# A reordered front and first half blocks, a ring of two pairs of PSUM banks, modulation tiles in the scan, and copies one ahead in the FFN

## The chip, the cores and the metric

The kernel runs on one core of a Trainium2 chip. The metric is device time in microseconds (us) of one execution. Five engines run side by side, each through its own list of instructions in order: TensorE (PE in the rows, PEld for its weight loads), VectorE (DVE), ScalarE (ACT), GpSimd (POOL) and SyncE (SP, which only issues DMAs). They wait for each other by semaphores. Matmul results land in PSUM, eight banks of 128 partitions x 512 floats; all else is in SBUF.

## The reference

One layer of a diffusion transformer with an S5 mixer, in float32: 1024 latent tokens and 256 context tokens of width 1024.

```python
m_l = split(silu(c) @ ada_w + ada_b, 6)              # modulation of the latent tokens
m_c = split(silu(c_ctx) @ ada_w + ada_b, 6)          # and of the context tokens
h_l = rms_norm(x, norm_mix) * (1 + m_l[1]) + m_l[0]; h_c = (the same of ctx with m_c)
# S5: 64 groups of 16 channels, 64 complex states each, in two directions;
# the latent scan starts from the context's last state
lam_bar = exp(lam * exp(log_step)); b_bar = (lam_bar - 1) / lam * b
state[t] = lam_bar * state[t-1] + b_bar @ u[t];  y[t] = Re(c_mat @ state[t])     # both directions added
g = gelu(y + d_skip * h_l);  x = x + m_l[2] * (g * sigmoid(g @ w_glu + b_glu))
h = rms_norm(x, norm_ffn) * (1 + m_l[4]) + m_l[3]
x = x + m_l[5] * ((silu(h @ w1) * (h @ w3)) @ w2)    # hidden width 2816
out = rms_norm(x, norm_final)
```

## The kernel before

Time is cut into 160 chunks of 8 tokens (32 of context, 128 latent). Instructions run on each engine in the order of the Python code: nothing is rescheduled, so moving a call moves its instructions on every engine that it uses. The stages are these.

**Front.** DMAs bring `x`, the context (`ctxT`) and the first 16 modulation tiles. ACT squares ten pieces of the tokens into a ring `junk` of two buffers, POOL folds each, and PE sums them (L184). Meanwhile DVE works out `lam_bar`, its powers `PW` and the input factors `CP` (`cmul`). PE spreads `CP` over the partitions (`dup`, L289) and the result is evicted as the table `LB` (L313, L77). `ada1(h, k)` (L282) accumulates the rows of shift and scale in the bank `prow`; `mix_rows` turns them (L411, L414), and `mix_cols` makes columns `cols` and `colp` of them (L426, L427). With these `rs_lat`, `u_lat`, `u_act` and `u_ctx` normalise and modulate the inputs `U`, eight groups at a time (`b` = 0 to 7).

**Sums.** A loop over 16 half blocks, `hb` = 2*b + d (d is the direction). Each needs input weights: `bl_make(hb)` multiplies `LB` with the matrices `BXY` into two parts (on POOL for the numbers in `PMUL`, else on DVE, which then reads a copy of the `LB` slice that `lb_psum` puts into PSUM by ACT). `bl_sum` adds the parts by an accumulating DMA from POOL's queue; below `NPE` PE adds them instead (L397, L398). `bl_tr` transposes them through PSUM (L400) into the ring `Win` (L401). `sums(hb)` multiplies the weights with `U` (L516), and ACT evicts the results into the state buffer `STQ` (L521 for d = 0, L523 and L524 for d = 1). All of these take turns in one PSUM ring `pw` of three banks. `pair` and `ctx_tree` combine neighbouring chunks by rotations (`rot`, on DVE or POOL). `power8` and `powers` square `lam_bar` up to the larger strides, and `pw_full` spreads `PW` (L289, L350). Between the blocks `ada` (L470) accumulates the second part of the modulation, 64 tiles of 256 KB in the bank `pm`; the first 32 of them stand in this loop.

**Scan.** `ctx_last`, then `scan()` on DVE: 32 coarse steps, fills, 63 fine steps. Meanwhile `run(prog)` goes through a written-out list of words for the other engines: `A`n takes tiles up to number n, `C` makes output matrices (POOL, for the first four with PE, L602), `K` and `T` the Toeplitz kernels by way of DRAM (L713 to L731), `M` turns the second modulation (L778, L782), `L` and `G` load and sign the matrices `Cs`, `F` fills on POOL, `R` restacks states (L819), `P` multiplies (L837, L842) and `Y` evicts (L894).

**GLU and FFN.** Then come the gate with the last restacks, and 22 hidden tiles of the FFN in split precision (L1209 to L1211). The first two are plain; for the rest the seven combinations of `h` in `BV` are prepared by `t3_steps`, `t24_steps` and `t1_steps` beside tiles 0 and 1. Such a step copies an operand into a PSUM bank of a ring of two by ACT (L1266, L1278, L1285), DVE adds, and `t_split` casts by ACT (L1151) and subtracts on POOL. `up_plain` advances them (`rest`) between its matmuls.

Most DVE and POOL operations are recorded by the helper `tt` and have its line, L70.

```python
for hb in range(16):
    sums(hb)
    ...
    elif hb < 13:
        bl_tr(hb + 3)
    ...
HOW = ((PE,) * 4,) + ((SY,) * 4,) * 3
run("A40 C00 A44 C01 A48 C02 A52 C03 A56 A60 A64 K0 K1 L2 C10 C11 M0 M1 C12 T0 ...")
```

Of the kernel before, what the change touches and what calls it, by code (L numbers as in the profile page):

```python
# [17 lines left out]
P = 128  # L18
# [19 lines left out]
def s5_ffn_kernel(tc, a, out):  # L38
# [3 lines left out]
    with ctx:  # L42
# [80 lines left out]
        def pw(shape=(4, P)):  # L123
            return pA.tile([P] + list(shape), F32, tag="w", name="pw", bufs=3)

        prow = pA.tile([P, 512], F32, tag="r3", name="prow")
        pm = pA.tile([P, 512], F32, tag="r2", name="pm")
        V.memset(prow, 0.0)
        V.memset(pm, 0.0)
# [8 lines left out]
        ctxT = view(RA, 13.5, [G, 32])  # L138
# [21 lines left out]
        LTa = pA.tile([P, 512], F32, tag="r0", name="lta")  # L160
        LTb = pA.tile([P, 512], F32, tag="r1", name="ltb")
        lbt = pA.tile([P, 512], F32, tag="r4", name="lbt")

# [13 lines left out]
        junk = [view(RC[3], 8 + 4 * i, [2, 512]) for i in range(2)]  # L177
        psx, psc = pw([4, P]), pw([16, 32])
        for i in range(10):
            src = X[:, 8 * i:8 * i + 8] if i < 8 else ctxT[:, 32 * i - 256:32 * i - 224]  # L180
            jk, po = junk[i % 2], psx if i < 8 else psc
            S.activation(jk.rearrange("p a b -> p (a b)").rearrange("p (g c) -> p g c", c=src.shape[2]), src, AF.Square)
            tt(jk[:, 0], jk[:, 0], jk[:, 1], ADD, E)
            PE.matmul(po.rearrange("p g c -> p (g c)"), blk, jk[:, 0], start=i % 8 == 0, stop=i in (7, 9))  # L184
# [112 lines left out]
        V.tensor_reduce(rsx, psx.rearrange("p g c -> p c g"), AX.X, ADD)  # L297
        cmul(PW[:, 2:3], PW[:, 0:1])
        V.tensor_copy(yb, PW[:, 3])
        cmul(CP[:, 4:6], CP[:, 0:2])  # L300
        cmul(CP[:, 6:8], CP[:, 2:4])
        V.tensor_reduce(rsc, psc.rearrange("p g c -> p c g"), AX.X, ADD)
        S.activation(rsb, rsb, AF.Sqrt, bias=epsc[:, 0:1], scale=1.0 / D)
        LB = view(RC[2], 8, [2, T, P])
        for n in range(4):
# [4 lines left out]
            if n % 2:  # L310
                ts(o, pt, sgn[:, 0:1] if i else 1.0, MUL)
            else:
                S.activation(o, pt, AF.Copy, scale=sgn[:, 0:1] if i else 1.0)  # L313
        for k in range(3):
            ada1(0, k)
        cmul(PW[:, 7:8], PW[:, 3:4])
# [4 lines left out]
        def power8():  # L321

            pt = pw([2, 4, 2, 8])
# [10 lines left out]
        def powers(*ps_):  # L334

            t2 = view(RXc, 3, [2, G])
            for p in ps_:
                i_, o = SQ[p], SQ[p + 1]
                if p == 1:
                    V.tensor_copy(LQ[p], i_)  # L340
                j_ = LQ[p] if p < 2 else i_
                tt(t2, i_[:, 0:2], j_[:, 0::2], MUL)
                stt(o[:, 1], i_[:, 0], -2.0, j_[:, 2], MUL, MUL)
                stt(o[:, 2], i_[:, 0], 2.0, j_[:, 2], MUL, MUL)
                tt(o[:, 0], t2[:, 0], t2[:, 1], ADD)

        def pw_full(n):
            pt = pw()
            dup(pt, lambda d: PW[:, 2 * n:2 * n + 2].rearrange("p t i g -> p (t i) g"))
            S.copy(PWF[:, 2 * n:2 * n + 2].rearrange("p t i g -> p (t i) g"), pt)  # L350
# [4 lines left out]
        BL2 = [view(r, kb, [8, T, HC]) for r, kb in ((RC[1], 12), (RXc, 4), (RC[3], 4), (RA, 22), (RA, 26), (RA, 30), (RA, 34))]  # L355
        Win = [view(RC[r], kb, [4, P]) for r, kb in ((3, 0), (3, 2), (2, 0), (2, 2), (2, 4), (2, 6))]
# [17 lines left out]
        def lb_psum(*hbs):  # L374

            for hb in hbs:
                n, o = {1: (0, 0), 3: (0, 128), 4: (1, 384), 7: (0, 0), 9: (0, 128), 11: (1, 384), 12: (2, 384), 14: (0, 0),
# [11 lines left out]
        def bl_tr(hb):  # L389
            b, d = divmod(hb, 2)  # L390
            t1, t2 = bls(hb)
            for j in range(2):
                pt = pw()
                for i in range(4):
                    w = t1[:, 4 * j + i].rearrange("p s h -> p (s h)")
                    if hb < NPE:
                        PE.matmul(pt[:, i], w, ident, start=True, stop=False)  # L397
                        PE.matmul(pt[:, i], t2[:, 4 * j + i].rearrange("p s h -> p (s h)"), ident, start=False, stop=True)  # L398
                    else:
                        PE.transpose(pt[:, i], w, ident)  # L400
                S.copy(Win[(2 * hb + j) % 6], pt)  # L401
# [6 lines left out]
        r4, mx = view(RA, 38, [4, P]), view(RA, 40, [2, 2, 32])  # L408

        def mix_rows():  # L410
            S.copy(r4, prow.rearrange("p (m n) -> p m n", m=4))  # L411
            pt = pw()
            for m in range(4):
                PE.transpose(pt[:, m], r4[:, m], ident)  # L414
            return pt

        def mix_cols(h, pt):

            hs = slice(4 * h, 4 * h + 4)
# [5 lines left out]
            pcol = pw([2, 2, 32])  # L425
# [24 lines left out]
        NA = 24  # L450
        stg = [view(RA, kb, [512]) for kb in [74] + [42 + 2 * i for i in range(15)] + [60.5 + 2 * i for i in range(8)]]
        stg += [view(RC[2], 8 * (1 - i // 4) + 2 * (i % 4), [512]) for i in range(8)]
        ada_at = [0, 0]

        def ada_tile(i):
            return stg[i if i < NA else NA + (i - NA) % 8]
# [18 lines left out]
        lb_psum(1, 3, 4)  # L475
        power8()
        bl_make(0)
# [9 lines left out]
        ada1(0, 7)
        pt = mix_rows()
        bl_tr(1)
        mix_cols(0, pt)  # L490
        u_act(0, 0, 4)
        u_lat(0, 4)
        u_ctx(0)
        bl_make(3)
        rs_lat(1)
        tt(Xc[:, 16:], ctxT[:, 16:], bc(rcp, 1, G - 16), MUL)
        u_ctx(1)
        u_lat(1)
        SY.dma_start(BXY[:, 0], a["bxy"][:, 2])
        powers(0, 1)  # L500
        rs_lat(2)
        bl_make(4)
        bl_make(5)
        bl_sum(4)
        stt(KD.rearrange("p q g h -> p (q g) h"), bc(pat, 1, 16), 1.0, bc(dcol, 2, HC), MUL, MUL)
        tq = None


        def sums(hb):
            b, d = divmod(hb, 2)  # L510
            for j in range(2):
                w = Win[(2 * hb + j) % 6]
                for ri in range(2):
                    pv = pw([512])[:, 0:320].rearrange("p (e c) -> p e c", e=2)
# [999 lines left out]
```

## Time and profile before

| | |
|---|---|
| median of 3 runs | 1100.76 us (1095.19 to 1100.89) |
| the profiled execution | 1099.35 us |
| its span in the trace | 1097.1 us |
| mean granted clock of TensorE | 0.969 |
| busy: PE, DVE, ACT, POOL | 91%, 71%, 38%, 57% of the span |
| PE on the chain that ended last | 74% of the span |
| HBM read | 83.20 MB |

A row of the timeline gives start and duration in us, engine, line, operation, output and inputs with shapes, and in brackets the idle time of that engine just before and what ended it. Rows that stand next to each other and are alike are merged ("x4"). One float32 matmul of the program is two instructions in the trace. In rows of windows each engine's busy time stands in turn, then the granted clock, the share of the DMA engines' time and GB/s.

### The profile page before, as it was taken

How to read it: one execution, taken by the hardware profiler on the slowest of the kernel's cores; microseconds unless marked ns; L12 is line 12 of the kernel's file. 1: busy time of each engine (PE TensorE's matmuls, PEld its weight loads, DVE VectorE, ACT ScalarE, POOL GpSimd, SP SyncE). 2: the span in 40 equal slices, each digit the busy share in tenths (PEclk: the TensorE clock that was granted, in tenths of full speed). 3: DMA queues.
4: the chain of work that ended last, by engine and by line, in shares of the span. 5: the costliest groups of instructions: out<-in, count | busy, mean ns of one | idle time of the engine just before them, and what ended most of it. 6: DMA issues, size and time to landing. Idle time of an engine off the chain costs nothing.

```text
span 1097.1 us, 16934 instructions
## 1 busy us (share of the span) xinstructions
PE 1000.6 (91%) x6208; PEld 803.8 (73%) x6208; DVE 777.2 (71%) x1808; ACT 419.2 (38%) x880; POOL 621.8 (57%) x484
## 2 busy tenths in 40 slices
PE   5889897546999999699999999999999999999997
PEld 1546632435899997587888888888888888888875
DVE  7688989994665786588666666666666666666657
ACT  4338741543864574322222222222222222222236
POOL 4446787881273454656555555555555555555563
PEclk9989999777999999999999999999999999999999
DMA  9577778665324012001111111100111111111104
GB/s 340 210 207 154 198 238 218 166 126 126 110 95 131 22 34 83 19 1 59 58 58 58 58 58 58 54 28 35 58 58 58 58 58 58 59 58 58 52 27 153
DMA packets 54514, 103.04 MB, mean 94 GB/s; under 512 B 4384, under 2 KB 25120, under 8 KB 53408
## 3 DMA queue, kind: packets, MB, share of 16 engines
q1 hardware_dynamic: 46656, 85.57, 23.6%
q0 software_dynamic: 3456, 12.58, 6.2%
q10 hardware_dynamic: 4320, 3.81, 1.1%
q8 instruction: 49, 0.80, 0.3%
q14 instruction: 33, 0.27, 0.1%
HBM read 83.20 MB, written 6.16 MB: 81 GB/s over the span
## 4 chain that ended last, share of the span: by engine, by line
PE 74%; DMA 6%; ACT 6%; DVE 6%; POOL 5%; issue 2%; ACTq 0%; SPq 0%; POOLq 0%; DVEq 0%
PE pu L1211 11%; PE pu L1210 11%; PE pu L1209 11%; PE pd L1209 7%; PE pd L1211 7%; PE pd L1210 7%; PE pw L516 3%; PE pe L974 3%; PE pe L975 3%; PE pe L973 3%; POOL c L70 3%; DVE ru L70 2%; PE prow L282 2%; DMA rxc<-in_cxy 1%; PE pm L470 1%
## 5 line engine op out<-in xcount | busy, mean ns | idle before, releaser
L70 POOL TENSOR_TENSOR c<-rxc,c 128x512 fp32r<-128x512 f32 x128 | 166.9, 1319 | 186.9 <-ACT c L1151 179.8
L70 DVE TENSOR_TENSOR ru<-pd,ru 128x512 f32<-128x512 f32 x336 | 226.6, 689 | 0.6 <-PE pd L1211 0.5
L1209 PE MATMUL pu<-ra,c 128*128 128x512 f32 x432 | 169.0, 391 | 9.3 <-DVE ru L70 8.9
L1211 PE MATMUL pu<-ra,c 128*128 128x512 f32 x432 | 168.9, 391 | 0.6 <-POOL c L70 0.6
L1210 PE MATMUL pu<-ra,c 128*128 128x512 f32 x432 | 168.7, 390 | 0.6 <-DVE ra L70 0.6
L1151 ACT CAST c<-rxc 128x512 fp32r<-128x512 f32 x128 | 76.9, 617 | 189.2 <-POOL rxc L70 107.1
L1209 PE MATMUL pd<-c 128*128 128x512 f32 x336 | 131.1, 390 | 1.9 <-DVE ru L70 1.9
L1211 PE MATMUL pd<-c 128*128 128x512 f32 x336 | 130.7, 389 | 0.0
L1210 PE MATMUL pd<-c 128*128 128x512 f32 x336 | 130.7, 389 | 0.0
L70 DVE TENSOR_TENSOR ru<-pu,ru 128x512 f32<-128x512 f32 x84 | 57.8, 688 | 82.1 <-PE pu L1211 51.0
L1209 PEld LDWEIGHTS pu<-ra,c 128*128 128x128 f32 x432 | 81.5, 189 | 26.8 <-DVE ru L70 9.3
L70 POOL TENSOR_TENSOR c<-ru,c 128x1024 fp32r<-128x1024 f32 x22 | 52.9, 2405 | 82.5 <-ACT c L952 73.9
L1211 PEld LDWEIGHTS pu<-ra,c 128*128 128x128 f32 x432 | 81.4, 188 | 18.8 <-POOL c L70 1.9
L1210 PEld LDWEIGHTS pu<-ra,c 128*128 128x128 f32 x432 | 81.5, 189 | 17.8 <-POOL c L70 0.9
L1209 PEld LDWEIGHTS pd<-c 128*128 128x128 f32 x336 | 63.1, 188 | 16.1 <-DVE ru L70 3.1
L1209 PE MATMUL pu<-c,c 128*128 128x512 f32 x192 | 74.9, 390 | 0.0
L1211 PE MATMUL pu<-c,c 128*128 128x512 f32 x192 | 74.7, 389 | 0.0
L1210 PE MATMUL pu<-c,c 128*128 128x512 f32 x192 | 74.7, 389 | 0.0
L1211 PEld LDWEIGHTS pd<-c 128*128 128x128 f32 x336 | 63.1, 188 | 13.1
L1210 PEld LDWEIGHTS pd<-c 128*128 128x128 f32 x336 | 63.1, 188 | 12.9
L70 DVE TENSOR_TENSOR ru<-ru,rxa 128x512 f32<-128x512 f32 (+1 forms) x62 | 63.9, 1031 | 7.1 <-ACT ru L1363 3.1
L952 ACT CAST c<-ru 128x1024 fp32r<-128x1024 f32 x21 | 22.1, 1050 | 112.8 <-DVE ru L70 112.8
(329 smaller groups left out, 2222.0 us busy)
## 6 DMA issues: line engine op xcount, KB each, us to landing
ru<-in_w SPq DMA_DIRECT2D x22, 512.0 KB, 3.6
c<-in_ada_w SPq DMA_DIRECT2D x40, 256.0 KB, 5.1
rxc<-in_w SPq DMA_DIRECT2D x38, 256.0 KB, 4.5
rxc<-in_w SPq DMA_DIRECT2D x19, 512.0 KB, 5.3
c<-c POOLq DMA_DIRECT2D x18, 512.0 KB, 5.4
ra<-in_ada_w SPq DMA_DIRECT2D x24, 256.0 KB, 5.6
ra<-in_ada_w SPq DMA_DIRECT2D x10, 512.0 KB, 10.8
ru<-in_xT SPq DMA_DIRECT2D x4, 1024.0 KB, 6.1
```

Source lines behind the costliest of these rows:

```text
L70: eng.tensor_tensor(out=o, in0=x, in1=y, op=op)
L282: PE.matmul(prow[32 * i:32 * i + 2], scs[:, k], stage[h][k][:, b], start=k == 0, stop=k == 7, tile_position=(0, 32 * i))
L470: PE.matmul(pm[32 * b:32 * b + 2], sc3[:, k, 1 - h:3 - h], ada_tile(i), start=i < 4, stop=i >= 60, tile_position=(0, 32 * b))
L516: PE.matmul(pv[64 * (i % 2):64 * (i % 2) + 64, i // 2], w[:, i, 64 * ri:64 * ri + 64], U[:, 8 * b + 4 * j + i], start=True, stop=True)
L952: S.copy(hl[0], raw)
L973: PE.matmul(pz, h_[:, k], wH[:, k], start=n == 0, stop=False)
L974: PE.matmul(pz, h_[:, k], wL[:, k], start=False, stop=False)
L975: PE.matmul(pz, l_[:, k], wH[:, k], start=False, stop=n == 7)
L1151: S.copy(o[0], x)
L1209: PE.matmul(pu, wh, bh, start=start, stop=False)
L1210: PE.matmul(pu, wh, bl, start=False, stop=False)
L1211: PE.matmul(pu, wl, bh, start=False, stop=stop)
```

## The change

- **Front.** `junk` has six buffers instead of two, in another region; `ctxT` moves to the region `RXa` (it lay where the first states are written). The powers that `CP` needs come first on DVE, the reductions of the sums behind them, and `PW[2]` goes to the loop. All four evictions of `LB` are ACT's. All of `ada1(0, k)` and `mix_rows` stand ahead of `bl_tr(0)`, and the turned rows (`mix_turn`) and columns use the bank `prow` itself.
- **First half blocks.** `bl_tr(1)` to `bl_tr(5)`, `ada1(1, k)`, `powers`, `u_lat`, `u_ctx` and `rs_lat` are dealt to other blocks; `NPE` is 2 instead of 4, `bl_make(0)` is DVE's and `bl_make(3)` POOL's. `mix_cols(1)` moves from block 3 to block 5. `powers` takes one factor from PSUM in every product, and adds a PSUM and an SBUF operand.
- **PSUM ring.** From the first half block to the end of the sums the ring is of two tiles of two banks (`pv2`): one holds a whole `bl_tr`, or both parts of half a `sums`, and ACT evicts it by one instruction (d = 0) or two (d = 1), not two or four.
- **Modulation.** No tile of `ada` stands in the loop. Eight are loaded near its end, all 64 are multiplied during the scan, in a ring of 12 and then eight buffers. `pm` is allocated and cleared by DVE only after the loop.
- **FFN.** `t_next` copies the operands for `t3_steps` and `t24_steps` one ahead of their use.

Cut to its core:

```diff
-        junk = [view(RC[3], 8 + 4 * i, [2, 512]) for i in range(2)]
+        junk = [view(RC[1 + 2 * (i // 4)], 4 * (i % 4) + 8 * (i // 4), [2, 512]) for i in range(6)]
...
-        V.tensor_reduce(rsx, psx.rearrange("p g c -> p c g"), AX.X, ADD)
-        cmul(PW[:, 2:3], PW[:, 0:1])
         V.tensor_copy(yb, PW[:, 3])
         cmul(CP[:, 4:6], CP[:, 0:2])
         cmul(CP[:, 6:8], CP[:, 2:4])
+        for k in range(2):
+            ada1(0, k)
+        V.tensor_reduce(rsx, psx.rearrange("p g c -> p c g"), AX.X, ADD)
...
+        psW, pW = pool("psV")
...
-                tt(t2, i_[:, 0:2], j_[:, 0::2], MUL)
+                tt(t3, i_[:, 0], j_[:, 0], MUL)
+                tt(t2, i_[:, 1], j_[:, 2], MUL)
...
-                tt(o[:, 0], t2[:, 0], t2[:, 1], ADD)
+                tt(o[:, 0], t3, t2, ADD)
...
-        PMUL, NPE = (0, 2, 5, 6, 8, 10, 13), 4
+        PMUL, NPE = (2, 3, 5, 6, 8, 10, 13), 2
...
+            if hb >= NPE:
+                S.copy(w_.rearrange("p j i n -> p (j i n)"), pt.rearrange("p j n -> p (j n)"))
...
-                ada_load(min(i + 8, top))
+                ada_load(min(i + (12 if i < 4 else 8), top))
...
+                pv = pv[:, :, 0:320].rearrange("p r (e c) -> p c r e", e=2)
+                if d == 0:
+                    S.copy(st[:, 0:160, :, 0, e:e + 2], pv)
...
+        ADA1 = {0: (0,), 1: (1,), 2: (2, 3), 3: (4, 5), 4: (6, 7)}
+        BLTR = {0: (1,), 1: (2,), 2: (3, 4)}
...
+        psW, pW = pool("psX")
+        NW[0] = 3
+        pm = pW.tile([P, 512], F32, tag="m", name="pm")
+        V.memset(pm, 0.0)
         pair(15, E)
         ctx_tree(3, range(4), 12, 16)
         ctx_last()
...
-        run("A40 C00 A44 C01 A48 C02 A52 C03 A56 A60 A64 K0 K1 L2 C10 C11 M0 M1 C12 T0 ...
+        run("A8 A12 C00 A20 C01 A26 C02 A32 C03 A38 K0 A42 K1 A46 L2 C10 A50 C11 A54 A58 A64 M0 M1 C12 T0 ...
...
+        tq_, TSRC = [], [x for s in range(4) for x in ([(6, s)] if s < 2 else []) + [(0, s), (1, s)]]
+        def t_next():
+            while len(tq_) < 2 and TSRC:
+                j, s = TSRC.pop(0)
+                tq_.append(pt_())
+                S.copy(tq_[-1], f32s(hl(BV[j], s))[0])
+            return tq_.pop(0)
```

Three places of the order, before and now. On PE in the front, from the spreading of `CP` (L289, now L297) to the first transposes of weights (L397, now L410); the rows with `prow` and `2x512` are tiles of `ada1`. Before:

```order
L289 MATMUL pw<-ra,r_60 64x4x64 x16
L282 MATMUL prow<-c_66,r_60 2x512 x4
L282 MATMUL prow<-c_65,r_60 2x512 x2
L327 MATMUL pw<-ra,r_60 64x8x8 x4
L282 MATMUL prow<-c_65,r_60 2x512 x2
L282 MATMUL prow<-c_63,r_60 2x512 x4
L282 MATMUL prow<-ra,r_60 2x512 x2
L397 MATMUL pw<-r_60,c_64 128x128
```

Now:

```order
L290 MATMUL prow<-c_66,r_60 2x512 x4
L297 MATMUL pw<-ra,r_60 64x4x64 x16
L290 MATMUL prow<-c_65,r_60 2x512 x4
L290 MATMUL prow<-c_63,r_60 2x512 x4
L290 MATMUL prow<-ra,r_60 2x512 x4
L431 MATMUL prow<-r_60,ra 128x128 x4
L410 MATMUL pv<-r_60,c_64 128x128
```

All eight tiles of the first half, and the turning of the rows (L431), now stand ahead of the first weights, and `power8` (L327) behind them.

On PE behind the last `sums` (L516, now L524): `pm` rows are the second modulation, four tiles for each "x4", L602 (now L610) the first output matrices, `kt` the Toeplitz kernels. Before:

```order
L516 MATMUL pw<-ru,c_66 64x160 x16
L470 MATMUL pm<-c_65,r_60 2x512 x12
L602 MATMUL pw<-c_63,r_60 128x512
L602 MATMUL pw<-c_64,r_60 128x512
L602 MATMUL pw<-c_63,r_60 128x512
L602 MATMUL pw<-c_64,r_60 128x512
L470 MATMUL pm<-c_65,r_60 2x512 x4
```

Now:

```order
L524 MATMUL pv<-ru,c_66 64x160 x16
L485 MATMUL pm<-c_65,r_60 2x512 x4
L485 MATMUL pm<-c_64,r_60 2x512 x4
L485 MATMUL pm<-c_65,r_60 2x512 x4
L610 MATMUL pw<-c_63,r_60 128x512
L610 MATMUL pw<-c_64,r_60 128x512
L610 MATMUL pw<-c_63,r_60 128x512
L610 MATMUL pw<-c_64,r_60 128x512
L485 MATMUL pm<-c_65,r_60 2x512 x8
```

The first matrix has 12 tiles ahead of it and the second eight more, all tiles from number 0 on; before, it was tiles 28 to 39, and four.

On ACT at the end of hidden tile 0 and the start of tile 1 of the FFN: `ra<-r_60` are the casts of `t_split`, the 128x1024 cast splits the weights of `w2`, `pt` rows are the copies into PSUM. Before:

```order
L1220 CAST c_4432<-ru 128x512
L1151 CAST ra<-r_60 128x512 x3
L952 CAST c_4432<-ru 128x1024
L1266 COPY pt<-ra 128x512
L1151 CAST ra<-rxa 128x512
L1234 ACTIVATE ru<-pu 128x512
L1278 COPY pt<-c_2974 128x512
```

Now:

```order
L1276 COPY pt<-ra 128x512
L1159 CAST c_2943<-rxc 128x512
L1228 CAST c_4317<-ru 128x512
L1159 CAST ra<-r_60 128x512 x3
L960 CAST c_4317<-ru 128x1024
L1276 COPY pt<-c_2859 128x512
L1159 CAST ra<-rxa 128x512
```

The copy for the first step of the next token tile stands ahead of the three casts, and each later one a step earlier.

More of the change, by code (lines that the diff above doesn't have):

```diff
@@ L481, in s5_ffn_kernel @@
         tt(Xc[:, 0:16], ctxT[:, 0:16], bc(rcp, 1, 16), MUL)
-        bl_make(1)
+        lb_psum(0, 1)
         bl_make(2)
-        for k in range(3, 7):
-            ada1(0, k)
+        bl_make(0)
+        mix_rows()
+        mix_turn()
         bl_tr(0)
[L487 to L490, printed above, removed]
+        mix_cols(0)
         u_act(0, 0, 4)
@@ L639, in s5_ffn_kernel @@
[L639 to L647 removed]
+            for k in ADA1.get(hb, ()):
+                ada1(1, k)
+            if hb == 4:
+                mix_rows()
@@ L1283, in t24_steps @@
             yield
[L1284 to L1285 removed]
+            a_ = t_next()
             tt(a_, t2, a_, SUB)
```

230 lines of the change are left out of this document (107 added, 123 removed).

## The prediction

> **What bounds the kernel now.** I read the chain that ended last first, then the windows by stage, and then the timeline of one engine at a time where the windows show that engine nearly full or another one waiting for it. The chain, and the windows of front, half blocks, scan and the FFN from its third hidden tile on (columns: start and end, length, busy time and instructions of PE, PEld, DVE, ACT and POOL, granted clock, DMA share, GB/s):
>
> ```profile
> PE 74%; DMA 6%; ACT 6%; DVE 6%; POOL 5%; issue 2%; ACTq 0%; SPq 0%; POOLq 0%; DVEq 0%
> 0.00:52.60 52.60, 35.52 (x164) 16.18 (x164) 34.47 (x136) 20.90 (x32) 22.07 (x21) 1.00 0.79 287
> 52.60:145.00 92.40, 82.85 (x803) 58.10 (x806) 78.31 (x155) 60.84 (x177) 60.42 (x68) 0.93 0.70 178
> 145.00:285.00 140.00, 92.59 (x1200) 59.81 (x1196) 117.79 (x639) 56.82 (x131) 93.28 (x78) 0.84 0.67 173
> 507.00:1097.00 590.00, 581.75 (x2563) 480.59 (x2561) 391.99 (x564) 169.77 (x298) 322.58 (x235) 1.00 0.17 57
> ```
>
> The last row is PE at work without a break for 590 us; the change does not touch it. What can move lies before 507: the 52.6 us until the first `sums`, the loop, the scan, and some waits beside the first two hidden tiles. In the loop PE's 82.85 is the modelled duration of many small overlapping matmuls; the stalls stand on DVE's list, 78.31 busy with the stalls below in between, so I count the loop by DVE.
>
> **Front.** Timeline rows from the squares to the first sums:
>
> ```profile
> 9.75 3.78 PE L184 MATMUL pw<-c,r 128*128 128x512 f32 x4 [9.75 <-POOL c L70]
> 26.32 0.69 DVE L297 TENSOR_REDUCE r<-pw 128x128 f32<-128x512 f32 x1 [2.86 <-PE pw L184]
> 28.77 1.13 PE L184 MATMUL pw<-c,r 128*128 128x512 f32 x2 [0.57 <-POOL c L70]
> 30.12 0.49 DVE L70 TENSOR_TENSOR ra<-lta,rxc 128x128 f32<-128x128 f32 x2
> 30.47 3.67 PE L289 MATMUL pw<-ra,r 128*64 128x256 f32 x32 [0.56 <-DVE ra L70]
> 34.19 0.75 DVE L77 TENSOR_SCALAR c<-pw,r 128x512 f32<-128x512 f32 x1 [1.04 <-PE pw L289]
> 38.75 1.21 DVE L70 TENSOR_TENSOR c<-c,lbt 128x1024 f32<-128x1024 f32 x1
> 40.66 0.49 PE L397 MATMUL pw<-r,c 128*128 128x128 f32 x2
> 51.20 1.65 ACT L442 ACTIVATE ru<-ru,r 128x128 f32<-128x128 f32 x4
> 52.61 2.86 PE L516 MATMUL pw<-ru,c 128*64 128x160 f32 x24 [1.78 <-POOL ru L70]
> ```
>
> A product of `CP` ends the wait of `dup` (30.12, 30.47). On DVE the reduce stands ahead of it and waits 2.86 for squares. With `CP` first, the 2.86, the reduce (0.69) and `PW[2]` (0.8, an estimate from two overlapping ops of 0.49) leave its way: ready at 30.6 - 4.4 = 26.2, `dup` until about 31 behind the squares on PE, `LB` evicted by 32.3. The squares: four instructions are two matmuls, so 1.89 each, ten from 9.75 end at 28.65 (before 29.9) if the ring of six lets ACT run ahead of POOL. The reduce then ends at 28.65 + 1.04 + 0.69 = 30.4; behind it stand the reciprocals, `rs_lat`, the modulation's product and both products of `bl_make(0)` (two of 1.21; the rest some ten small ops, estimated at 3.2 by 0.49 and less for one), so the weights are there at 35.9 instead of 40.66. From there the old list has `bl_tr(0)`, `bl_tr(1)`, rows of `ada1`, `mix_rows` and `u_act` up to 52.61; now `ada1` and `mix_rows` are past, `bl_tr(1)` goes behind `sums(0)`, and what stays is `bl_tr(0)` (estimated at 3.6, eight times the row at 40.66), the columns (two such rows, 1.0) and `u_act` (1.65): 42.2. **Gain 10.4.** If the tiles of `ada1`, now ahead of the first weights on PE, come late by DMA (0.79 of the DMA time is in use here), half of it is lost; so 5 to 12.
>
> The row at 9.75 has 0.95 per instruction, the one at 28.77 0.57. The Trainium skill ("TensorE: Matmul & The Clock Gate", "What's actually happening") says that the array starts at half rate and comes to full rate after one busy window of some 3.4 us. By that rule an unbroken run of squares would be fast from at most 16.6 on and end near 23.6, which as an estimate makes the front 1.9 us shorter than by the row at 9.75. The sum keeps the row's pace for all ten.
>
> **Half blocks.** DVE's stalls, a normal op of the slow one's shape, and POOL beside it:
>
> ```profile
> 59.81 0.22 DVE L70 TENSOR_TENSOR rxa<-rxc 128x64 f32<-128x64 f32 x1
> 65.47 6.04 DVE L70 TENSOR_TENSOR rxc<-rxc 128x64 f32<-128x64 f32 x2
> 66.14 4.64 POOL L70 TENSOR_TENSOR c<-c,c 128x1024 f32<-128x1024 f32 x2
> 60.06 0.36 DVE L340 COPY lta<-rxa 128x192 f32<-128x192 f32 x1
> 77.30 1.22 DVE L70 TENSOR_TENSOR c<-c,lbt 128x1024 f32<-128x1024 f32 x1 [4.76 <-ACT lbt L382]
> 92.06 2.35 DVE L70 TENSOR_TENSOR c<-c,lbt 128x1024 f32<-128x1024 f32 x2 [3.73 <-ACT lbt L382]
> 143.22 0.43 DVE L70 TENSOR_TENSOR ltb<-ra,lta 128x256 f32<-128x256 f32 x1 [1.81 <-ACT ra L521]
> L521 ACT COPY ra<-pw 128x320 f32<-128x320 f32 x32 | 13.5, 446 | 7.4 <-DVE ru L70 4.3 <-PE pw L516 1.4 <-ACT lbt L382 0.3
> ```
>
> The op at 65.47 reads two operands from SBUF while POOL runs, and ends as POOL's product does: 6.04 for what is 0.22 elsewhere. With one operand in PSUM this stall of 5.8 goes. The waits of 4.76 and 3.73 are for the copies of `LB` by ACT, whose list had evictions of weights ahead; dealt out otherwise, they go too: 14.3 in all. Against it: one such wait of about 4.3 stays, since in the new order the `LB` copy for block 7 stands behind two lots of `Win`; `PW[2]` (1.2) and two copies more of 0.36 come into the loop, 1.9; I set 2.4 for new small waits beside the 1.81, which stays. Net 5.7, bounds 3 (another wait of the kind) to 12. `bl_make(3)` for `bl_make(0)` on POOL, and accumulating DMAs in place of PE's sum for two half blocks, stand in POOL's list, with 60.42 busy of 92.40: nothing, as long as they are half a block ahead; if not, 4 us, the wait of the rows above. The ring of two pairs saves ACT an instruction in two; at 446 ns each it costs nothing unless PE waits for the eviction (rival B).
>
> Front and loop together: the scan begins 10.4 + 5.7 = **16 us earlier** (8 to 23), 140 instead of this row:
>
> ```profile
> 155.96 0.29 DVE L70 TENSOR_TENSOR ltb<-ra,lta 128x128 f32<-128x128 f32 x1
> ```
>
> **Scan.** Here the tiles that the loop no longer has must pass. `pm` is cleared some 4 us ahead of the scan, at 136; about 56 of the 64 tiles then come by DMA, and the list has them ahead of `M0`. Before (PE's, SP's, window, and the waits further on):
>
> ```profile
> 140.61 36.11 SPq L463 DMA_DIRECT2D c<-in_ada_w  x35
> SPq L463 <- PE pm L470: 40.1, 9, 23.1
> 154.24 3.70 PE L602 MATMUL pw<-c,r 128*128 128x512 f32 x8
> 140.00:180.00 40.00, 35.97 (x171) 12.34 (x168) 36.91 (x192) 10.97 (x28) 32.26 (x23) 1.00 0.82 265
> 177.64 3.88 PE L470 MATMUL pm<-c,r 128*2 128x512 f32 x11 [2.37 <-DMA c<-in_ada_w]
> 190.15 1.12 PE L782 MATMUL pw<-r,c 128*128 128x128 f32 x4 [3.88 <-ACT c L778]
> 194.69 1.39 POOL L70 TENSOR_TENSOR c<-ra,r 128x256 f32<-128x256 f32 x2 [5.59 <-DVE ra L70]
> 194.59 0.38 PE L713 MATMUL kt<-c,c 128*16 128x112 f32 x2 [2.84 <-DMA c<-c]
> 231.45 0.37 PE L713 MATMUL kt<-c,rxa 128*16 128x112 f32 x2 [3.59 <-DMA c<-c]
> 257.50 0.28 PE L713 MATMUL kt<-c,rxa 128*16 128x112 f32 x2 [1.19 <-DMA c<-rxc]
> ```
>
> A tile is two instructions. Price of one: 0.71 at the fast end (11 in 3.88, behind a wait for DMA), 1.03 at the slow end (35 issues in 36.11), 0.99 for 262 KB at 265 GB/s. I take the 0.99, since the stretch is the same and the DMA share was 0.82: 56 x 0.99 = 55.4, tile 64 at 191.4, and `M0`'s turn at 192.0, 1.9 later than the 190.15 of before, though DVE is 16 earlier. `K0`, `K1`, `C10` and `C11` now go ahead of it. Behind it, the waits for POOL's matrices shrink, as POOL (whose 5.59 for DVE at 194.69 shows it ahead there) is earlier: 2.84 at 194.59, then 3.59 at 231.45 and 1.19 at 257.50. PE's and ACT's path thus ends the stage at +1.9 - 2.84 - 3.59 - 1.19 = -5.7: of the 16, **5.7 stay and 10.3 are given back**. At 0.71 tile 64 is there at 176 and all of the 16 stay; at 1.03, 3.4 stay.
>
> By the Trainium skill ("DMA: Bandwidth & Descriptors", "Where 436 GB/s comes from") loads from HBM are bound at about 358 GB/s for a core; an estimate by that is 0.73 us a tile, which would let the whole 16 stand. The row with 265 GB/s is below it; the 0.71 of the row at 177.64 lies at it.
>
> **FFN.** Rows around the end of hidden tile 0:
>
> ```profile
> 435.37 0.50 PE L1209 MATMUL pd<-c 128*128 128x512 f32 x1 [1.62 <-DVE ru L70]
> 449.38 1.05 ACT L952 CAST c<-ru 128x1024 fp32r<-128x1024 f32 x1
> 450.94 0.69 DVE L70 TENSOR_TENSOR pt<-ra,pt 128x512 f32<-128x512 f32 x1 [4.64 <-ACT pt L1266]
> 454.83 0.69 DVE L70 TENSOR_TENSOR pt<-rxa,pt 128x512 f32<-128x512 f32 x1 [1.67 <-ACT pt L1278]
> 465.55 0.69 DVE L70 TENSOR_TENSOR pt<-r,pt 128x512 f32<-128x512 f32 x1 [1.17 <-ACT pt L1278]
> 466.90 0.79 PE L1209 MATMUL pu<-ra,c 128*128 128x512 f32 x1 [8.92 <-DVE ru L70]
> ```
>
> DVE's chain to PE's start at 466.90 has one wait of 4.64 and five from 1.67 to 1.17 in it. With the copy ahead of the casts the first goes; the second step then waits for the cast at 449.38 and its own copy, until about 451.0 instead of 454.83 (3.8 won). Of four more waits of 1.2 I take 2.8 of 4.8, since ACT still has 1.2 of work for each step: 6.6. Of the 1.62 at 435.37, which ends the same kind of chain, 1.2. **Gain 7.8**, bounds 3.8 to the 10.5 that PE waits at all.
>
> **The sum.** 16 - 10.3 + 7.8 = 13.5. The profiled execution took 1099.35, so 1085.9; the median of the runs shown, 1100.76, stands 1.4 above it. I say 1086, by itself from 1080 to 1092. A measurement can tell about 0.5%, 5.5 us, from no change.
>
> **The rivals.**
> A. The tiles cost nothing: at 0.71 the stream is there before `M0` is due. 1099.35 - 16 - 7.8 = 1075.6. For it: the row at 177.64, and 40.1 us in which SP waited for PE and not the reverse. Against it: the share of 0.82. Chance 0.20.
> B. The ring of two pairs ties PE to ACT: `sums` has a pair free only when ACT has evicted the whole of the last one. ACT has 60.84 in the loop; 16 half blocks with one eviction of 446 ns uncovered are 7.1 us of the 16, none of which returns in the scan: 1093. For it: L521 waited 4.3 us for PE, so both are close. Chance 0.15.
> C. Slower: the stream stops while PE stands in output matrices and Toeplitz kernels, because SP waits for PE's release of buffers (the 23.1 in one wait). Four matrices of 3.70, and `K0` and `K1` with the 4.8 between the end of the row at 177.64 and the beginning of PE's idle 3.88, then add 20 to the 55.4: tile 64 at 211, the stage ends 14 later than before in place of 5.7 earlier, and the time is 1099.35 + 14 - 7.8 = 1106. It decides from tile 64 at 205 on, 1.23 us a tile. Against it: a ring of eight is 8 us of tiles, more than one matrix. Chance 0.10.
> D. Nothing gained in sum: the stage takes back the whole 16, by a stream of 1.09 us a tile, and the FFN copies win 3.8 only: 1095. Chance 0.12.
>
> **How the numbers follow.** The forecast has 0.43. Faster by over 0.5% are forecast, A and B: 0.78; within it D, 0.12; slower C, 0.10. The range from 1070 (A with 5 more from the bounds of front and loop) to 1096 takes in A, B and D and leaves C and the ends out.
>
> **What would show it.** First `sums` near 42 and no DVE wait for the reduce's squares ahead of `CP`; no 6 us op in the loop; scan's first step at 140; last `pm` matmul at 191 and the Toeplitz wait of 3.59 gone; PE's idle of 8.92 down to about 2. Wrong it is if the last `pm` matmul comes at 176 (A) or behind 205 (C), or if PE's idle time in the loop is put down to evictions (B).

## The result and the profile after

| | before | after |
|---|---|---|
| median, five runs each | 1099.56 us (1095.19 to 1100.89) | 1090.71 us (1089.14 to 1094.96) |
| ratio of after to before, 95% interval | | 0.9929 (0.9900 to 0.9959) |
| the profiled execution | 1099.35 us | 1094.96 us |
| its span | 1097.1 us | 1093.1 us |

The change makes the kernel 0.7% faster, about 8 us, where the prediction said 13.5. The profiled execution of after is the longest of its five, so its trace shows only 4.4 of the 8. The time is inside the range, but in part by luck: of the four terms of the sum two had the wrong size and a third brought nothing, and what the FFN gave beyond its term made up for a part of that.

The chain that ended last, by engine and by line, on the page of after:

```profile
PE 70%; DVE 12%; DMA 6%; POOL 6%; ACT 3%; issue 2%; SPq 0%; ACTq 0%; POOLq 0%; DVEq 0%
PE pu L1219 11%; PE pu L1218 11%; PE pu L1217 11%; PE pd L1217 7%; PE pd L1218 7%; PE pd L1219 7%; POOL c L70 3%; DVE ru L70 3%; PE pe L982 3%; PE pe L983 3%; PE pe L981 3%; PE pm L485 2%; DMA c<-in_ada_w 2%; DVE c L70 2%; DVE ra L70 2%
```

The modulation tiles, `pm` and their loads, stand in it with some 45 us (25 before, by the pieces of the chain). Timeline rows of after, from the squares to the first sums:

```profile
9.66 8.38 PE L192 MATMUL pw<-c,r 128*128 128x512 f32 x12 [9.66 <-POOL c L70]
21.94 2.35 PE L192 MATMUL pw<-c,r 128*128 128x512 f32 x4 [0.85 <-POOL c L70]
26.66 3.67 PE L297 MATMUL pw<-ra,r 128*64 128x256 f32 x32 [0.56 <-DVE ra L70]
43.67 2.41 PE L524 MATMUL pv<-ru,c 128*64 128x160 f32 x32 [1.39 <-POOL ru L70]
```

`dup` (L297) starts at 26.66 instead of 30.47, the sums at 43.67 instead of 52.61. Next the loop and the beginning of the scan, DVE and then PE. The row at 143.72 is the clearing of `pm`, the one at 148.33 the scan's first step:

```profile
65.05 1.22 DVE L70 TENSOR_TENSOR c<-c,lbt 128x1024 f32<-128x1024 f32 x1 [7.41 <-ACT lbt L394]
135.17 0.43 DVE L70 TENSOR_TENSOR ltb<-ra,lta 128x256 f32<-128x256 f32 x1 [6.00 <-ACT ra L529]
143.72 0.48 DVE L693 MEMSET pm<- 128x512 f32 x1
148.33 0.29 DVE L70 TENSOR_TENSOR ltb<-ra,lta 128x128 f32<-128x128 f32 x1
144.26 4.55 PE L485 MATMUL pm<-c,r 128*2 128x512 f32 x24 [7.69 <-DVE pm L693]
```

The slow op beside POOL is gone, and so are the waits of 4.76 and 3.73. In their place DVE waits 7.41 and 6.00. The loop, from first sums to the scan's first step, took 103.35 before and takes 104.66 now. The wait of 6.00 is longer in this execution than in others: the runs below that leave this loop as it is have 3.2 to 4.1 there, and loops of 102.4 to 103.5. PE then stands 7.69 for DVE's clear. The scan stage, first by two windows (busy time of PE, its weight loads, DVE, ACT and POOL, then granted clock, DMA share and GB/s):

```profile
160.00:180.00 20.00, 17.25 (x180) 6.22 (x171) 20.00 (x115) 3.17 (x7) 14.88 (x9) 1.00 0.94 295
180.00:200.00 20.00, 11.61 (x71) 2.12 (x72) 20.00 (x116) 0.72 (x2) 12.51 (x15) 0.66 1.02 292
```

The tile `pm` in the view of one tile (least, median and longest ns of one instruction, then the first and last start in us):

```profile
L485 PE MATMUL pm<-c,r x128: 589/592/1061, 144.3 to 206.6; 128*2 128x512 f32 x128
```

And the timeline: ACT's turn of the modulation, POOL's waits for output matrices (the first two of its rows are from the kernel before), and the last Toeplitz matrices, which stood at 257.50:

```profile
207.21 0.59 ACT L785 COPY c<-pm 128x512 f32<-128x512 f32 x1 [21.16 <-PE pm L485]
164.19 5.99 POOL L70 TENSOR_TENSOR c<-rxc,rxa 128x1024 f32<-128x1024 f32 x3 [2.12 <-PE pw L602]
173.54 3.98 POOL L70 TENSOR_TENSOR c<-rxc,rxa 128x1024 f32<-128x1024 f32 x2 [2.20 <-PE pw L602]
152.59 4.01 POOL L70 TENSOR_TENSOR c<-rxc,rxa 128x1024 f32<-128x1024 f32 x2 [2.67 <-PE pw L610]
159.63 5.98 POOL L70 TENSOR_TENSOR c<-rxc,rxa 128x1024 f32<-128x1024 f32 x3 [3.04 <-PE pw L610]
171.31 3.98 POOL L70 TENSOR_TENSOR c<-rxc,rxa 128x1024 f32<-128x1024 f32 x2 [4.53 <-PE pw L610]
264.10 0.28 PE L720 MATMUL kt<-c,rxa 128*16 128x112 f32 x2 [1.55 <-DMA c<-rxc]
```

The last tile is multiplied at 206.6 (181.4 before), ACT stands 21.16 for it, and what stood at 257.50 stands at 264.10: a scan stage that began 7.6 earlier ends 6.6 later. In the chain that ended last, tiles and matrices follow each other on PE from 144 to 166 without a load; behind that, three loads stand in it with 18 us, and PE stands once for a Toeplitz kernel whose store took 7.7 (the chain's rows, then PE's timeline):

```profile
166.65 6.17 DMA c<-in_ada_w
187.32 6.59 DMA c<-in_ada_w
196.92 5.23 DMA c<-in_ada_w
184.48 0.58 PE L720 MATMUL kt<-c,c 128*16 128x112 f32 x8 [5.96 <-ACT r L729]
```

The FFN, PE and DVE:

```profile
441.23 0.50 PE L1217 MATMUL pd<-c 128*128 128x512 f32 x1 [0.40 <-DVE ru L70]
464.15 0.50 PE L1217 MATMUL pu<-ra,c 128*128 128x512 f32 x1 [0.35 <-DVE ru L70]
456.81 0.70 DVE L70 TENSOR_TENSOR pt<-rxa,pt 128x512 f32<-128x512 f32 x1 [2.51 <-ACT pt L1276]
```

PE's idle times of 1.62 and 8.92 are 0.40 and 0.35. Of DVE's waits for these copies between the two rows of PE, one of 2.51 is left.

### The profile page after: what moved, and what is told of

Its sections match the earlier page's. It is cut to its first block, busy times and chain, and to the rows that moved or that the text cites. A ratio compares the mean times of both kernels' runs of the same rounds, so it can differ in the third digit from the quotient of the medians.

```text
span 1093.1 us, 16750 instructions
## 1 busy us (share of the span) xinstructions
PE 995.3 (91%) x6160; PEld 797.9 (73%) x6160; DVE 772.9 (71%) x1811; ACT 413.0 (38%) x818; POOL 626.0 (57%) x486
## 4 chain that ended last, share of the span: by engine, by line
PE 70%; DVE 12%; DMA 6%; POOL 6%; ACT 3%; issue 2%; SPq 0%; ACTq 0%; POOLq 0%; DVEq 0%
PE pu L1219 11%; PE pu L1218 11%; PE pu L1217 11%; PE pd L1217 7%; PE pd L1218 7%; PE pd L1219 7%; POOL c L70 3%; DVE ru L70 3%; PE pe L982 3%; PE pe L983 3%; PE pe L981 3%; PE pm L485 2%; DMA c<-in_ada_w 2%; DVE c L70 2%; DVE ra L70 2%
## 5 line engine op out<-in xcount | busy, mean ns | idle before, releaser
L70 POOL TENSOR_TENSOR c<-rxc,rxa 128x1024 f32<-128x1024 f32 x30 | 62.0, 2128 | 17.6 <-PE pw L610 10.2
```

The lines of the kernel that those rows point to most:

```text
L70: eng.tensor_tensor(out=o, in0=x, in1=y, op=op)
```

## The experiments

Each ran in five rounds beside the kernel before; ratios are to it.

**1. The FFN alone, and all but the FFN.** The first is the kernel before with `t_next`, the second the changed kernel with

```diff
-                a_ = t_next()
+                a_ = pt_()
+                S.copy(a_, b12[0])
```

and the same at the two places in `t24_steps`.

> The kernel before with nothing but the copies one ahead in the FFN. Theory F (PE stood behind DVE's chain of copies, and those waits are the whole of what the FFN can give): PE's idle of 8.92 and 1.62 shrink to under 1 each, and the time falls by 9 to 11.5, to 1088 to 1091, about the whole of what the change brought. Rival G (the FFN gained in the changed kernel only because its stages meet in another phase there): under 4, so 1096 or more, with a wait of 4 or more left ahead of PE's 466.

> The changed kernel with the FFN's copies as they were before. Theory F: the front, the loop and the scan together bring nothing, since all that the earlier start of the sums won is given back in loop and scan: 1098 to 1103, and PE's idle of about 9 ahead of hidden tile 1 is back. Rival G: 1093 to 1096, front and scan do bring 4 or more.

Measured 0.9897 (0.9878 to 0.9917) and 1.0041 (1.0026 to 1.0056). The FFN's copies alone are worth 11 us, more than the whole change, and everything else together makes the kernel 4.5 us slower; PE's wait ahead of hidden tile 1 is back there with 7.51. The two add up to the changed kernel's 0.9929 (1.0041 - 0.0103 = 0.9938). PE's rows of the FFN alone:

```profile
432.41 0.50 PE L1209 MATMUL pd<-c 128*128 128x512 f32 x1 [0.39 <-DVE ru L70]
455.31 0.50 PE L1209 MATMUL pu<-ra,c 128*128 128x512 f32 x1 [0.29 <-DVE ru L70]
```

The same waits are gone without any other part of the change: theory F holds in both directions.

**2. The operands of `powers` alone.** On the kernel before (the copy into PSUM stands for the third and fourth power, whose `LQ` has no bank yet; `t3` is a slice of a PSUM bank):

```diff
-                tt(t2, i_[:, 0:2], j_[:, 0::2], MUL)
+                if p > 1:
+                    j_ = lbt[:, 256:448].rearrange("p (r e) -> p r e", e=G)
+                    V.tensor_copy(j_, i_)
+                tt(t3, i_[:, 0], j_[:, 0], MUL)
+                tt(t2[:, 0], i_[:, 1], j_[:, 2], MUL)
...
-                tt(o[:, 0], t2[:, 0], t2[:, 1], ADD)
+                tt(o[:, 0], t3, t2[:, 0], ADD)
```

> The kernel before with nothing but one operand of each product, and one of each sum, of powers in PSUM (two copies of 0.36 more). Theory V (DVE bounds the loop): the op of 6.04 beside POOL's product falls to under 0.5, the scan begins about 5 earlier, and the time falls by 4 to 5, to about 1094. Rival N (the next wait takes it): the wait of 4.76 for ACT's copy of LB at 77 grows to 8 to 10, the scan's first step moves by under 1.5, the time by under 2.

Measured 1.0000 (0.9986 to 1.0014). DVE's rows: the sum that was slow, an op behind it, the next wait, and the scan's first step; then two of ACT's, an eviction of weights and the copy that DVE waits for.

```profile
65.46 0.22 DVE L70 TENSOR_TENSOR rxc<-lbt,rxc 128x64 f32<-128x64 f32 x1
66.91 3.45 DVE L70 TENSOR_TENSOR c<-c,ra 128x128 f32<-128x128 f32 x1
76.61 1.22 DVE L70 TENSOR_TENSOR c<-c,lbt 128x1024 f32<-128x1024 f32 x1 [6.26 <-ACT lbt L387]
155.53 0.29 DVE L70 TENSOR_TENSOR ltb<-ra,lta 128x128 f32<-128x128 f32 x1
74.04 0.59 ACT L406 COPY c<-pw 128x512 f32<-128x512 f32 x1 [4.16 <-PE pw L403]
76.31 0.28 ACT L387 COPY lbt<-c 128x128 f32<-128x128 f32 x1
```

The sum's stall is gone, and nothing moves. The row of 6.04 is two ops, of which the slow one took 5.41; now it is 0.22. But 3.2 of it came back at once: the op at 66.91, 0.28 elsewhere, reads two operands from SBUF and ends as the same two products of POOL do. And the wait for ACT's copy grew from 4.76 to 6.26, not to the 8 to 10 that N said, since part of the stall had only moved. DVE goes on at 76.61 instead of 77.30, and the scan starts at 155.53 instead of 155.96; the first sums are 0.7 earlier too. ACT made that copy as long after the first sums as before, 24.4, since evictions of weights stand ahead of it and wait 4.16 for PE, whose list has no idle time from 60 to 78. Rival N holds: the busy engine's stall was slack that another engine's chain covered.

**3. FFN, `powers` and `CP` first on the kernel before.** On top of the FFN's copies and the edit of experiment 2:

```diff
-        V.tensor_reduce(rsx, psx.rearrange("p g c -> p c g"), AX.X, ADD)
-        cmul(PW[:, 2:3], PW[:, 0:1])
         V.tensor_copy(yb, PW[:, 3])
         cmul(CP[:, 4:6], CP[:, 0:2])
         cmul(CP[:, 6:8], CP[:, 2:4])
+        V.tensor_reduce(rsx, psx.rearrange("p g c -> p c g"), AX.X, ADD)
+        V.tensor_copy(yb, PW[:, 1])
+        cmul(PW[:, 2:3], PW[:, 0:1])
+        V.tensor_copy(yb, PW[:, 3])
```

> The kernel before with the FFN's copies one ahead, the operands of powers in PSUM, and the powers of CP ahead of the reduction of the sums on DVE; tiles, ring and deal of the blocks as before. Theory V: 4 from the front and 4 to 5 from the loop on top of the 1087.5 of the FFN alone: 1078 to 1081. Rival N: both are given back in the loop at waits for ACT and at the tiles, 1084 to 1088.

Measured 0.9897 (0.9878 to 0.9916), the same as the FFN alone. The scan's first step, here and then with the FFN alone:

```profile
151.23 0.30 DVE L70 TENSOR_TENSOR ltb<-ra,lta 128x128 f32<-128x128 f32 x1
```

```profile
153.83 0.29 DVE L70 TENSOR_TENSOR ltb<-ra,lta 128x128 f32<-128x128 f32 x1
```

It is 2.6 earlier, of the expected 8 (0.3 of it from the front: first sums at 50.21 and 50.52), and in the median nothing reaches the end. Rival N again.

**4. The two new waits of the loop.**

```diff
+            if hb == 2:
+                lb_psum(7)
             for n in BLTR.get(hb, (hb + 2,)):
...
-            if hb + 5 in (7, 9, 11, 12, 14, 15):
+            if hb + 5 in (9, 11, 12, 14, 15):
...
-        BLTR = {0: (1,), 1: (2,), 2: (3, 4)}
+        BLTR = {0: (1,), 1: (2,), 2: (3, 4), 13: (), 14: (15,)}
```

> The changed kernel with the LB copy for block 7 ahead of two evictions of weights on ACT, and bl_tr(15) behind sums(14) instead of ahead. Theory V (DVE waited 7.41 and 6.00 there, and DVE carries the loop and pm's clear): the first wait falls to 3 to 5 (then the accumulating DMA of block 4 is due), the second to under 2, pm's clear and scan 6 earlier, and the time by 4 to 6, to 1085 to 1087. Rival N: other waits of the loop take it, the scan's first step under 2 earlier, time within 2 of 1090.7.

Measured 0.9890 (0.9874 to 0.9906), 1085.7, 4 to 5 us better than the changed kernel (0.9929; the intervals touch). The two waits and the scan's first step in DVE's timeline, and the tile:

```profile
60.69 1.22 DVE L70 TENSOR_TENSOR c<-c,lbt 128x1024 f32<-128x1024 f32 x1 [2.96 <-ACT lbt L394]
128.49 0.43 DVE L70 TENSOR_TENSOR ltb<-ra,lta 128x256 f32<-128x256 f32 x1 [1.67 <-ACT ra L529]
141.65 0.29 DVE L70 TENSOR_TENSOR ltb<-ra,lta 128x128 f32<-128x128 f32 x1
```

```profile
L485 PE MATMUL pm<-c,r x128: 589/592/1061, 137.6 to 198.8; 128*2 128x512 f32 x128
```

Most of both waits is gone, and scan and clear come 6.7 earlier than in the profile of after, 5.4 earlier than in that of the changed kernel again (experiment 8): theory V, for what the order of two instructions did here. It also shows the size of the give-back. This kernel's scan begins 12.2 ahead of that of the FFN alone (153.83), and its time is within 2 us of it.

**5. The clear of `pm` on ACT.**

```diff
-        V.memset(pm, 0.0)
+        S.activation(pm, cpk[:, 0:1].to_broadcast([P, 512]), AF.Copy, scale=0.0)
```

> The changed kernel with the bank pm cleared by ACT behind its last eviction, not by DVE behind its rotations. Theory S (the stream of tiles is late because it starts late: PE waited 7.7 for DVE's clear): first pm matmul at 138 instead of 144.3, the first output matrix on PE and so POOL about 6 earlier, last pm matmul at about 200 instead of 206.6, and 4 to 6 less in all, 1085 to 1087. Rival D (the loads themselves set the end of the stream, whose DMA share is near 1 from 160 on): the last pm matmul stays at 203 or later, and the time within 2 of the changed kernel's 1090.7.

Measured 0.9890 (0.9869 to 0.9912), 1086.75. The tile:

```profile
L485 PE MATMUL pm<-c,r x128: 589/592/1061, 136.7 to 202.7; 128*2 128x512 f32 x128
```

The stream starts 7.6 earlier than in the profile of after and ends 3.9 earlier (6.3 and 2.7 against the changed kernel again, 143.0 to 205.4). Both theories are half right: the time is theory S's, so the late clear cost about 4, and the last tile, at 202.7, comes near rival D's 203. That the loads took the rest of the early start is read from this, not tested here.

**6. Only 12 tiles loaded.**

```diff
-                SY.dma_start(ada_tile(i), adaw[k * P:(k + 1) * P, c0:c0 + 512])
+                if i < 12:
+                    SY.dma_start(ada_tile(i), adaw[k * P:(k + 1) * P, c0:c0 + 512])
```

> The changed kernel with only the first 12 modulation tiles loaded; the other 52 matmuls read what lies in the ring, so the second modulation is wrong, and 13.6 MB less are read. Theory S (loads set the scan stage): last pm matmul at 180 or before instead of 206.6, ACT's wait of 21 for it gone, K6 at 250 or before, and 9 to 13 less, 1078 to 1082. Rival O (the order on PE and DVE sets it, pm's late clear and output matrices behind tiles): the last pm matmul earlier, but POOL's first waits for the output matrices stay at 2 to 4 each and the time falls by under 5, 1086 or more.

Measured 0.9860 (0.9842 to 0.9879), about 8 less than the changed kernel. The tile, the window that had 292 GB/s, and POOL's three waits for output matrices, the last of which had 4.53:

```profile
L486 PE MATMUL pm<-c,r x128: 589/592/1057, 143.2 to 178.4; 128*2 128x512 f32 x128
```

```profile
180.00:200.00 20.00, 7.47 (x175) 6.35 (x174) 20.00 (x115) 3.84 (x10) 10.80 (x15) 0.60 0.56 119
```

```profile
151.27 4.00 POOL L70 TENSOR_TENSOR c<-rxc,rxa 128x1024 f32<-128x1024 f32 x2 [2.44 <-PE pw L611]
156.73 5.99 POOL L70 TENSOR_TENSOR c<-rxc,rxa 128x1024 f32<-128x1024 f32 x3 [1.46 <-PE pw L611]
167.57 4.01 POOL L70 TENSOR_TENSOR c<-rxc,rxa 128x1024 f32<-128x1024 f32 x2 [3.69 <-PE pw L611]
```

The other 52 matmuls read what lies in the ring, so the result is not the layer's. With the same 64 matmuls the stream takes 35 us instead of 62: the loads set its length, theory S, if short of its 9 to 13, and the last Toeplitz matrices are 8.8 earlier, not 14. POOL's three waits for output matrices add up to 7.6 here (2.44, 1.46 and the 3.69), to 10.2 with the change, to 4.3 before. Read so, 3.3 of the 5.9 more are the order on PE and its late start, which this run leaves as they were, and the rest is the loads.

**7. The last tiles behind `K2` and `K3`.**

```diff
-        run("... L2 C10 A50 C11 A54 A58 A64 M0 M1 C12 T0 T1 T2 T3 C13 F10 F11 G2 B3 B2 K2 K3 L3 C20 ...
+        run("... L2 C10 A50 C11 A54 C12 T0 T1 T2 T3 C13 F10 F11 G2 B3 B2 K2 K3 A58 A64 M0 M1 L3 C20 ...
```

> The changed kernel with the last 10 tiles and the turning of the second modulation (M0, M1) behind K2 and K3 in the list, still ahead of C20, whose place in SBUF the tiles use. Theory W (ACT and PE stand behind M0: ACT waited 21.2 for the last tile): R0's restacks start 8 to 12 earlier than 217, and the time falls by 3 to 6, to 1085 to 1088. Rival P (POOL's C20 waits for the tiles' place anyway, and its matrices end the stage): restacks earlier, but C20 still at 208 to 210 and K6 at 261 to 265, the time within 2 of 1090.7, or above it where the tiles now wait for K2.

Measured 0.9983 (0.9969 to 0.9997): 6 us slower than the changed kernel, worse than both theories' main case. The tile, and POOL's wait for `C20`'s place:

```profile
L485 PE MATMUL pm<-c,r x128: 589/592/1061, 142.0 to 211.1; 128*2 128x512 f32 x128
```

```profile
213.15 4.00 POOL L70 TENSOR_TENSOR c<-rxc,rxa 128x1024 f32<-128x1024 f32 x2 [8.44 <-PE pw L789]
```

The tiles end at 211.1, and POOL's `C20`, whose output lies where the last tiles and the turned rows lie, waits 8.44 for them. Rival P, with the delay that it named: POOL's matrices behind the tiles end the stage, not ACT's restacks, which did come 3.6 earlier (213.64 for 217.26).

**8. Both mendings, and the changed kernel again.** Experiments 4 and 5 in one kernel, and the changed kernel a second time beside it.

> The changed kernel with both mendings together: pm cleared by ACT, the LB copy for block 7 early, bl_tr(15) behind sums(14). Theory S (start of the stream and of the scan each cost their own piece): clear at about 133 and last pm matmul at about 196, time 1081 to 1084. Rival R (both act on the same piece, the start of the stream, which the second already moved 6.7 earlier by moving DVE): no better than 1085 to 1087, the time of either.

> The changed kernel once more, beside the others of this call: 1089 to 1092 by its first runs. If it were 1087 or less here, the 4 to 5 of the two mendings would be within what differs from chip to chip.

Measured 0.9909 (0.9892 to 0.9926) for both mendings and 0.9929 (0.9905 to 0.9952) for the changed kernel again; its 1091.7 is not the 1087 or less that would have made the single mendings' gain a difference from chip to chip. The tile, and POOL's second output matrix, of the kernel with both:

```profile
L485 PE MATMUL pm<-c,r x128: 589/592/1061, 133.6 to 201.0; 128*2 128x512 f32 x128
```

```profile
155.46 5.98 POOL L70 TENSOR_TENSOR c<-rxc,rxa 128x1024 f32<-128x1024 f32 x3 [6.06 <-PE pw L610]
```

The mendings do not add. The tiles start at 133.6, 4 earlier than with the loop's mending alone, and end at 201.0, 2 later. The second output matrix stands behind tile 20 on PE; PE reaches the tiles before their loads are there (9.3 us in six waits), and POOL waits 6.06 for that matrix. Rival R.

**9. Evictions of the sums in two.**

```diff
-                    S.copy(st[:, 0:160, :, 0, e:e + 2], pv)
+                    for ri in range(2):
+                        S.copy(st[:, 0:160, ri, 0, e:e + 2], pv[:, :, ri])
```

> The changed kernel with every eviction of sums for d = 0 in two instructions of one bank's part each, as before the change, the ring of two pairs kept: 16 evictions of 708 ns become 32 of about 450. Theory B (a pair comes free late and holds PE, and PE holds the loop): scan's first step 2 to 4 later, time 1092 to 1095. Theory L (the loop is held by the chain of input weights and the LB copies on ACT, not by evictions of sums): scan's first step within 1, time within 2 of the changed kernel's.

Measured 0.9935 (0.9914 to 0.9955), the changed kernel's time. The scan's first step on DVE:

```profile
145.26 0.29 DVE L70 TENSOR_TENSOR ltb<-ra,lta 128x128 f32<-128x128 f32 x1
```

The scan's first step is not later (145.26; 146.1 to 148.3 in five profiles of kernels with the loop as it was): theory L. The number of evictions for d = 0 is no term of the loop.

**10. Four more tile buffers.** On top of experiment 4, four tiles in the place of `BXY`, a first ring of 16, and loads asked for in blocks 11, 12 and 14:

```diff
-            return stg[i] if i < 12 else (stg[:4] + stg[8:])[(i - 12) % 8]
+            return stg[i] if i < 16 else (stg[4:8] + stg[12:])[(i - 16) % 8]
```

> The changed kernel with the two mendings of the loop (LB copy for block 7 early, bl_tr(15) behind sums(14); pm still cleared by DVE) and four more tile buffers, in the place of BXY, free from block 10 on: 12 tiles asked for in the loop instead of 8, and a ring of 16 at the start. Theory S (what has to be loaded during the scan sets the stream's end: 56 tiles took 61 us, none took 35): the last pm matmul about 4 earlier against the clear than the 61.8 with the two mendings alone, time 1081 to 1084. Rival D (DMA engines are the bound from the loop's end on and the four tiles only displace other transfers there): the distance from clear to last matmul within 1.5 of 61.8, time 1085 to 1087.

Measured 0.9915 (0.9895 to 0.9936). The tile, and POOL's matrices:

```profile
L485 PE MATMUL pm<-c,r x128: 589/592/1061, 137.9 to 200.6; 128*2 128x512 f32 x128
```

```profile
139.91 19.81 POOL L70 TENSOR_TENSOR c<-rxc,rxa 128x1024 f32<-128x1024 f32 x10 [3.83 <-PE pm L485]
```

From first to last matmul it is 62.7 instead of 61.2, rival D, though its 1085 to 1087 was passed by 1.5: four tiles fewer to load after the loop do not shorten the stream, and POOL now waits 3.83 because its first matrix is written where the first tiles lie.

| kernel | ratio, 95% | `pm`, first and last matmul |
|---|---|---|
| the change | 0.9929 (0.9900 to 0.9959) | 144.3 to 206.6 |
| FFN alone | 0.9897 (0.9878 to 0.9917) | as before |
| all but the FFN | 1.0041 (1.0026 to 1.0056) | 142.1 to 203.9 |
| loop mended | 0.9890 (0.9874 to 0.9906) | 137.6 to 198.8 |
| `pm` cleared by ACT | 0.9890 (0.9869 to 0.9912) | 136.7 to 202.7 |
| both | 0.9909 (0.9892 to 0.9926) | 133.6 to 201.0 |

No version is surely better than the FFN's copies alone, though the two single mendings (0.9890 each) lie below the change itself.

## Why the prediction was right and where it was not

**Front: right, a little short.** Said 10.4, measured 8.9 (43.67 against 52.61), and 0.7 to 2.1 of it are the execution: the FFN alone and `powers` alone, with the front as it was, have their first sums at 50.52 and 51.89. There only the first four instructions of the squares took 0.95 each and the others 0.56, with gaps like those of before, where twelve took 0.95. So the row at 9.75 was no price for all ten squares. In after they end at 24.3 and not at 28.65: twelve instructions take 8.38, 0.70 each in the mean. `dup` starts at 26.66, as worked out. Here the rule of the Trainium skill that the sum had left aside ("TensorE: Matmul & The Clock Gate", "What's actually happening") came nearer, with its estimate of 23.6.

**Half blocks: the step that failed.** "So I count the loop by DVE" was wrong. Said 5.7 less, measured 1.3 more, or between 0.9 less and 1.3 more over five profiles with this loop. The step priced each of DVE's stalls as if it were on the path: 5.8 + 4.76 + 3.73 (the first is 5.2 by itself, since the row of 6.04 holds two ops). Before, DVE was hardly on the path: of the 93 us from 52 to 145 the chain that ended last has 72 on PE and 5 on DVE. In after it has 47 on DVE, 16 on PE and 14 on DMA. Experiment 2 took the first stall away and moved the scan by 0.4. What DVE waits for there is ACT's copy of `LB`, and that copy is held by evictions of weights that wait for PE, so a DVE that is early only waits longer. The prediction saw one such wait of 4.3 remain; in the profile of after it is 7.41, and a second of 6.00 came from `bl_tr(15)`, which stands ahead of `sums(14)` and in that profile waits 2.39 for an accumulating DMA. Experiment 4 shows that these two, not the stalls of before, were worth something.

**Scan: the mechanism right in part, the size off.** The tiles did come late and the stage did take back the earlier start, but the prediction let PE's and ACT's path end it; by experiment 7 it is POOL's matrices, which wait for the tiles' place. Said tile 64 at 191.4 and 10.3 given back; measured 206.6 and 14.2 (7.6 earlier at the start, 6.6 later at 264.10). Of the 15.2 that the tile is later, 8.3 come from the start (144.3 for 136, since loop and clear are late) and 6.9 from the pace: 62.3 for 56 tiles is 1.11 each, not 0.99. The price came from a window at 265 GB/s as if all of it were tiles, but the matrices' accumulations and the Toeplitz stores share the DMA engines: at a share of 1.02 there were 292 GB/s for all. The 358 GB/s of the Trainium skill's page ("DMA: Bandwidth & Descriptors", "Where 436 GB/s comes from") were not reached in any window of the scan. Rival A, tiles for nothing, is refuted. Rival C's sign of the forecast being wrong, a last tile behind 205, came true at 206.6, and its mechanism is there in small: PE stands 5.96 in a Toeplitz kernel at 184.48, with 12 loads 0.6. Only the FFN keeps the kernel from being slower: without its copies it is (1.0041). Rival D had the stage right, at 1.09 a tile: all of the earlier start is taken back, and more (14.2 against 7.6). It had the FFN's 3.8 wrong. The 1090.7 lies midway between the forecast's 1086 and D's 1095, and that it is no worse is the FFN's doing.

**FFN: right, too small.** Said 7.8, measured 11 alone (experiment 1). The step "Of four more waits of 1.2 I take 2.8 of 4.8" held some back for ACT; all four went, and with them PE's idle times but for 0.75 of 10.54.

**The ring: as said, as far as tested.** Twice as many evictions for d = 0 cost nothing (experiment 9), so rival B's price of 7.1 falls. PE's waits for evictions of sums in the loop are 7.0 in all with the change and 5.0 before, and the changed loop with a ring of single banks was not run. The ring is also tied to the term that lost most: two pairs, the tables and `prow` are all eight banks, so there is none for `pm` during the loop, and the tiles can only be multiplied behind it. That the ring forces this is read from the code; a kernel with both the ring and `pm` in the loop was not tried.

**The sum.** By the trace -8.9 + 1.3 + 14.2 - 11.0 = -4.4, the difference of the two profiled executions (the 11.0 is what the other three leave; experiment 1 measured the same); said -10.4 - 5.7 + 10.3 - 7.8 = -13.6, 13.5 with its rounding. The medians differ by 8.9.

**Open.** With 12 loads only, the stage still gave some of its earlier start back, with POOL waiting for output matrices behind `pm` on PE. How much of the 14.2 is that order and how much the loads was bounded (the loads are 8 in time), and split only by POOL's waits as above; no run moved the order alone. That two good mendings do not add is shown; that the place of the second matrix behind tile 20 is the cause is only read from the trace.

## What to carry to other kernels

Removing a stall on a busy engine is a gain only if what the engine waits for next is early too: follow the next wait back to its own engine before the stall is priced. Work moved from a stage with room into a stage whose DMA is already near full is paid there, whatever it frees; here it took back more than front and loop had won. Try the parts alone: the smallest edit, two operands copied one step ahead, was worth more than all of it together.

## What the runs showed of the hardware

A DVE op of 0.22 that read two operands from SBUF while POOL ran a product took 5.41, and 0.22 again with one operand in PSUM; then the next op with two operands in SBUF took 3.45 instead of 0.28, until the end of the product. This is what the Trainium skill states ("SBUF — State Buffer", "SBUF: two separate sides"): a port pair shared by the two engines is locked for a whole instruction; the trace agrees.

The DMA engines had a share of 1.02 with 292 GB/s in the scan, and 0.93 with 335 GB/s in the first 45 us of the same kernel (the view of windows again):

```profile
0.00:45.00 45.00, 30.18 (x152) 13.77 (x154) 33.33 (x129) 20.55 (x32) 19.30 (x20) 1.00 0.93 335
```

A share near 1 is not one rate. That the mix of transfers sets it is likely, but no run here tested it.

The first matmuls of an execution can be slow for a time that differs from one execution to the next: in two profiles of one and the same front, with the same gaps, twelve and four instructions of the squares took 0.95 each before the others took 0.56.
